# Latents of the last four row tiles on VectorE, up-projection weights and V scales prepared a step ahead

## The chip, the core and the metric

The kernel runs on one core of one Trainium2 chip. A core has TensorE (PE; its weight loads are shown apart as PEld), VectorE (DVE), ScalarE (ACT), GpSimd (POOL) and SyncE (SP, which here issues every DMA). Each engine works through its own queue in order; engines wait for one another through semaphores. On-chip data lie in SBUF (128 partitions), matmul results in eight PSUM banks of 128 x 512 float32. The metric is the device time of one execution in microseconds (us), as the median of several runs.

## The reference

One encoder layer on a sequence of 1024 rows of width 1024, float32:

```python
mod = silu(c) @ w_ada + b_ada                    # shift, scale, gate for both halves
h = rmsnorm(x) * (1 + scale) + shift
q_lat, kv_lat, k_rope, ca_qkv = split(h @ w_in)  # 256, 128, 32, 3*8*64 columns
q  = rmsnorm(q_lat) @ w_q_up                     # 8 heads x 96
kv = rmsnorm(kv_lat) @ w_kv_up                   # 8 heads x (64 key + 64 value)
k  = concat(kv keys, k_rope for every head)      # 96 = 64 + 32
q, k = rmsnorm(q), rmsnorm(k); rotary on the last 32
o_mla = chunk-causal softmax attention(q, k, v)            # 8 heads
o_ca  = banded chunk attention(rmsnorm(cq), rmsnorm(ck), cv) + relative bias   # 8 heads
x = x + gate_a * (concat(o_mla, o_ca) @ w_out)
u = causal depthwise conv(modulated rmsnorm(x) @ w_up)
x = x + gate_m * ((silu(u_gate) * u_val) @ w_down)
```

## The kernel before

Every float32 product is made of three matmuls: a matrix is split into a high part (rounded) and a low part (the remainder), and high x high, high x low and low x high are added in PSUM. `hi_of` makes the high part (line 78 on ACT), `lo_of` the remainder (line 85, on POOL with `"p"`, on DVE with `"v"`). So each weight tile costs a load, one rounding and one subtraction ahead of its matmuls.

The program is written as streams that a scheduler merges. The main stream runs 64 attention tiles of the banded heads (units `c00` to `c31`) and then 64 of the latent heads (`m00` to `m13`): scores on PE (lines 814 and 821), a maximum on DVE, the exponential on ACT (line 846), scaling and splitting of the probabilities on POOL (line 74, tile `hl`) and DVE (line 868), a transposing DMA (line 880, `PT<-hl`), and the product with the values on PE (line 908). Between them a list of generators, the fillers, gives PE other work: `f_v` (values of the banded heads), `f_qk`, `f_m` (the latents), `f_up(0)` and `f_up(1)` (the up-projections of four latent heads each), `f_oca`. A pacing rule decides how many filler steps are recorded behind each attention tile; a list scheduler then puts all instructions into the queue of each engine by priority and by its own estimate of time. So the written order is not the order of the queues, and an edit in one filler moves instructions of its neighbours.

The part in question:

- `f_m` makes the latents in eight row tiles t. Tile `mp_t` is 24 matmuls (128 x 416, lines 155 to 157); ACT copies it into `lat_t` (line 514) and squares it (518 to 520); POOL makes the reciprocal root `mr_t` (lines 521, 120, 121), scales the two latents with it (523, 524) and rotates the shared key part (`rope_apply`, 498 to 501). After four tiles PE transposes the scaled latents, three pages of four blocks (line 531, bank `lt_ps`); ACT and DVE split each page (534, 535) into `latT`. Tag `T` has a single PSUM bank (`TB = 1`); tag `mm` has two.
- `f_up(gr)` loads the two weight tiles `wqr` and the tile `wkr`, splits them into `wq` and `wk` (ACT, then POOL), and makes the scale of the values: a sum of squares on ACT (line 649), then `pow2_scale`, which goes from DVE (323) to PE (325, tile `vspm`), DVE (326), POOL (328) and DVE again. Then for each of eight tiles t: `qu` (six matmuls), `ku` (three), their copies and squares on ACT (667 to 689), sums and rotation on DVE (673 to 695), the roots and the scaled key on POOL (120, 121, 694).
- `f_v(pp)` makes the same kind of scale (`vspc`) for the banded heads' values, after the first projection `ipv`.

Tag `A` is a ring of four SBUF tiles, which `f_ada` (a stream of modulation weights) and the loads of the output weights, `wor`, use; a load into it waits until the tile four allocations earlier has been read.

## Time and profile before

| | |
|---|---|
| runs | 1309.72 us median of 3 (1309.15 to 1316.19) |
| the profiled execution | 1314.38 us, of which the profile's span is 1312.6 us |
| PE busy | 1195.0 us (91%), 6168 matmuls |
| DVE busy | 1071.0 us (82%) |
| ACT, POOL busy | 624.9 us (48%), 600.2 us (46%) |
| TensorE clock granted, mean | 0.963 |

Up to about 600 us the program is attention with its fillers; after 700 us it is the channel half, in which PE is busy throughout. A busy share is an average over both halves: what a change between 60 and 600 us is worth is read from the waits there. The latents `mp` run from 257 to 330 us, the up-projections from 342 to 423 us.

### The profile page before, as it was taken

The numbers are of one execution on the slowest core, as the hardware profiler recorded it, in microseconds if no ns is written. First come the engines' busy times: TensorE is split into PE (matmuls) and PEld (weight loads), VectorE is DVE, ScalarE is ACT, GpSimd is POOL, SyncE is SP. The second block draws the span as 40 slices with busy tenths as digits, with TensorE's granted clock in tenths as the row PEclk, the third lists the DMA queues.
The fourth block names the chain that finished last, engine by engine and source line by source line (L and its number), as shares of the span: only waits on it lengthen the run. The fifth ranks groups of instructions, "written<-read, shape, count | busy, mean of one in ns | idle before, by whom it ended". The sixth has DMA issues, their size and how long they took to land. (4 is left out here: it accounts for less than half of the span.)

```text
span 1312.6 us, 18651 instructions
## 1 busy us (share of the span) xinstructions
PE 1195.0 (91%) x6168; PEld 992.1 (76%) x6168; DVE 1071.0 (82%) x1800; ACT 624.9 (48%) x1148; POOL 600.2 (46%) x639
## 2 busy tenths in 40 slices
PE   4899999989768889968989999999999999999998
PEld 3789888869546667756768888888888886888886
DVE  6979989878589678875899889888888987687667
ACT  5454654455567355543474444444444353433331
POOL 5485873587688544455615444544444441000000
PEclk9899999989889899988999999999999998999999
DMA  8416768666224757889603343333333338943441
GB/s 326 146 52 152 178 144 193 153 157 126 48 75 87 157 132 148 170 165 347 241 0 113 96 129 112 122 126 105 113 113 119 114 105 284 381 129 104 129 161 64
DMA packets 223689, 190.82 MB, mean 145 GB/s; under 512 B 148709, under 2 KB 166373, under 8 KB 223593
## 3 DMA queue, kind: packets, MB, share of 16 engines
q1 hardware_dynamic: 223592, 189.64, 51.3%
q8 instruction: 48, 0.79, 0.3%
q14 instruction: 49, 0.39, 0.1%
HBM read 117.50 MB, written 37.49 MB: 118 GB/s over the span
## 5 line engine op out<-in xcount | busy, mean ns | idle before, releaser
L78 ACT ACTIVATE dnP<-dnr 128x1024 fp32r<-128x1024 f32 x73 | 77.5, 1064 | 117.6 <-PE dnA_P L1484 46.4
L1456 DVE TENSOR_TENSOR dnP<-dnr,dnP 128x1024 fp32r<-128x1024 f32 x72 | 87.9, 1224 | 51.5 <-ACT dnP L78 50.0
L74 POOL TENSOR_SCALAR hlm<-Pm,rim 128x512 f16<-128x512 f32 (+3 forms) x96 | 69.5, 733 | 64.8 <-DVE rim L849 17.9
L85 POOL TENSOR_TENSOR wf<-wu,wf 128x512 fp32r<-128x512 f32 x22 | 38.7, 1758 | 116.3 <-ACT wf L78 116.3
L85 POOL TENSOR_TENSOR wb<-wu,wb 128x512 fp32r<-128x512 f32 x22 | 44.7, 2033 | 84.9 <-ACT wb L78 57.1
L821 PE MATMUL sm<-kp,qp 96*128 96x512 f32 (+7 forms) x288 | 71.2, 375 | 13.2 <-ACT Pm L846 11.8
L868 DVE SCALAR_TENSOR_TENSOR hlm<-Pm,rim,hlm 128x512 f16<-128x512 f32 (+3 forms) x96 | 70.6, 749 | 10.3 <-POOL hlm L74 10.1
L1318 DVE SCALAR_TENSOR_TENSOR u<-c,cvp,u 128x1023 f32<-128x1023 f32 x44 | 55.8, 1309 | 27.6 <-ACT u L1317 26.2
L74 POOL TENSOR_SCALAR hlc<-Pc,ric 128x640 f16<-128x640 f32 (+2 forms) x64 | 49.4, 775 | 44.1 <-DVE ric L849 12.9
L821 PEld LDWEIGHTS sm<-kp,qp 96*128 96x128 f32 (+1 forms) x288 | 49.1, 198 | 25.0 <-ACT Pm L846 16.7
L846 ACT ACTIVATE Pm<-sm,mm 128x128 f32<-128x128 f32 (+3 forms) x64 | 47.3, 739 | 38.8 <-DVE mm L839 23.4
L846 ACT ACTIVATE Pc<-sc,mc 128x640 f32<-128x640 f32 (+2 forms) x64 | 42.2, 660 | 49.4 <-DVE mc L836 28.0
L1317 ACT ACTIVATE u<-c,cvp 128x1024 f32<-128x1024 f32 x44 | 52.3, 1238 | 23.4 <-DVE c L1416 16.5
L868 DVE SCALAR_TENSOR_TENSOR hlc<-Pc,ric,hlc 128x640 f16<-128x640 f32 (+2 forms) x64 | 51.3, 808 | 7.8 <-POOL hlc L74 7.6
L78 ACT ACTIVATE wc<-ws 128x512 fp32r<-128x512 f32 x21 | 13.3, 632 | 92.9 <-DVE ws L1166 87.1
L908 PE MATMUL pvm<-PTm,vt 128*128 128x256 f16 (+1 forms) x320 | 42.9, 281 | 14.7 <-DMA PTm<-hlm 10.9
L155 PE MATMUL ipq<-wq_s,hT 128*128 128x256 f32 x192 | 56.0, 292 | 0.0
L1319 DVE SCALAR_TENSOR_TENSOR u<-c,cvp,u 128x1022 f32<-128x1022 f32 x44 | 55.5, 1300 | 0.0
L157 PE MATMUL ipq<-wq_s,hT 128*128 128x256 f32 x192 | 55.1, 287 | 0.0
L156 PE MATMUL ipq<-wq_s,hT 128*128 128x256 f32 x192 | 55.0, 287 | 0.0
L839 DVE TENSOR_REDUCE mm<-sm 128x1 f32<-128x128 f32 (+3 forms) x64 | 47.3, 746 | 9.3 <-PE sm L821 8.8
L908 PEld LDWEIGHTS <-vt 128*128 128x128 f16 x320 | 30.6, 103 | 28.8 <-issue 11.8
(436 smaller groups left out, 4385.1 us busy)
## 6 DMA issues: line engine op xcount, KB each, us to landing
wu<-w_up SPq DMA_DIRECT2D x44, 512.0 KB, 3.6
dnr<-g_d SPq DMA_DIRECT2D x73, 256.0 KB, 2.7
aw<-w_ada SPq DMA_DIRECT2D x48, 256.0 KB, 3.2
g_d<-u SPq DMA_DIRECT2D x22, 512.0 KB, 3.0
dnr<-w_down SPq DMA_DIRECT2D x44, 256.0 KB, 5.4
adaw<-w_ada_a SPq DMA_DIRECT2D x16, 512.0 KB, 6.1
x<-x SPq DMA_DIRECT2D x16, 512.0 KB, 8.9
g_d<-gs SPq DMA_DIRECT2D x22, 256.0 KB, 2.8
```

Source lines behind the costliest of these rows:

```text
L74: pool.tensor_scalar(o, i, s, 1.0, op0=MUL, op1=MUL)
L78: act.activation(o, i, AF.Copy)
L85: (pool if eng == "p" else dve).tensor_tensor(o, i, f32(hi), op=SUB)
L155: pe.matmul(pt, sh, mh, start=(start and i == 0), stop=False)
L157: last = pe.matmul(pt, sl, mh, start=False, stop=(stop and i == n - 1))
L821: last = pe.matmul(s[:, c:c + w], qpg[a][rr, q], kpgs[kh][rr, b, ko:ko + w], start=(a == 0 and b == 0), stop=(a == 1))
L846: act.activation(pr[:, :n], sv, AF.Exp, bias=m[:], scale=-1.0, accum_out=rsum[:, 0:1])
L868: dve.scalar_tensor_tensor(hl[:, w:2 * w], pp, ri[:], hl[:, :w], op0=MUL, op1=SUB)
L908: last = pe.matmul(dst, u.vst(j), mov, start=(x == 0), stop=(x == len(todo) - 1), skip_group_check=True)
L1318: dve.scalar_tensor_tensor(u[:, 1:], c[:, :S - 1], cvp[:, cv + 1:cv + 2], u[:, 1:], op0=MUL, op1=ADD)
L1319: dve.scalar_tensor_tensor(u[:, 2:], c[:, :S - 2], cvp[:, cv:cv + 1], u[:, 2:], op0=MUL, op1=ADD)
L1456: r = f(*a, **k)
```

## The change

Six edits:

1. `f_v`: `pow2_scale` is recorded ahead of the first projection, not behind it.
2. `f_m`, tiles 4 to 7: the two scalings and the key rotation go from POOL to DVE. `mr_t` stays on POOL.
3. `f_m`, second half: pages 1 and 2 of the transposed latents take banks of tag `mm`; page 0 stays in `T`.
4. A new function `up_prep(gr)` holds the loads of the up-projection weights and the scale of the values. It is called at tile 5 of `f_m` for `gr = 0`, and at tile 5 of `f_up(0)` for `gr = 1`.
5. Its loads go into the four tiles of ring `A`, where before they went into the two of ring `sq`.
6. For `gr = 0` the remainders of the two `wq` tiles are made on DVE, not on POOL.

```diff
         for t in range(0, NT, 2):   # f_v
...
-            pt = ps.tile([P, 512], F32, name=f"ipv{pp}_{t}", tag="mm", bufs=2)
-            yield from proj2(pt, t, w, 256)
             if t == 0:
                 vscale["c", pp] = pow2_scale(f"c{pp}", ssw[:], hb[:], ND, 2.0 * D)
                 sc = vscale["c", pp][0]
+            pt = ps.tile([P, 512], F32, name=f"ipv{pp}_{t}", tag="mm", bufs=2)
+            yield from proj2(pt, t, w, 256)
...
-            pool.tensor_scalar(raw[:, :QR], raw[:, :QR], r[:, 0:1], 1.0, op0=MUL, op1=MUL)
-            pool.tensor_scalar(raw[:, QR:QR + KVR], raw[:, QR:QR + KVR], r[:, 1:2], 1.0, op0=MUL, op1=MUL)
-            rope_apply(kr[:, t:t + 1, :], raw[:, QR + KVR:NM].unsqueeze(1), tabk, t, 1, raw[:, NM:NM + 64])
+            eng = dve if t >= NT // 2 else pool
+            eng.tensor_scalar(raw[:, :QR], raw[:, :QR], r[:, 0:1], 1.0, op0=MUL, op1=MUL)
+            eng.tensor_scalar(raw[:, QR:QR + KVR], raw[:, QR:QR + KVR], r[:, 1:2], 1.0, op0=MUL, op1=MUL)
+            rope_apply(kr[:, t:t + 1, :], raw[:, QR + KVR:NM].unsqueeze(1), tabk, t, 1, raw[:, NM:NM + 64], eng)
             lat[t] = raw
+            if t == NT - 3:
+                up_prep(0)
             if j == 3:
                 for b in range(3):
-                    ptt = ps.tile([P, 512], F32, name=f"lt_ps{h}_{b}", tag="T", bufs=TB)
+                    own = h == 1 and b > 0
+                    ptt = ps.tile([P, 512], F32, name=f"lt_ps{h}_{b}", tag="mm" if own else "T", bufs=2 if own else TB)
...
+    def up_prep(gr):
+        raws = []
+        for k in range(2):
+            raw = atile(f"wqr{gr}_{k}")
+            sp.dma_start(raw[:], I["w_qu"][gr][:, k, :])
+            raws.append(raw)
+        raw = atile(f"wkr{gr}")
+        sp.dma_start(raw[:], I["w_kvu"][gr])
+        raws.append(raw)
+        ssw = cst.tile([P, 1], F32, name=f"sswm{gr}")
+        junk = qtile(f"wkj{gr}")
+        act.activation(junk[:, 0:256].rearrange("p (a b) -> p a b", a=4),
+                       raw[:].rearrange("p (a b) -> p a b", a=4)[:, :, NOPE:], AF.Square, accum_out=ssw[:])
+        vscale["m", gr] = pow2_scale(f"m{gr}", ssw[:], gb2[:], 1, float(KVR))
+        upw[gr] = raws
...
-            raw = qtile(f"wqr{gr}_{k}")
-            sp.dma_start(raw[:], I["w_qu"][gr][:, k, :])
             w = g4([P, 2, 512], F32R, f"wq{gr}_{k}")
-            hi_of("a", w[:, 0], raw[:])
-            lo_of("p", w[:, 1], raw[:], w[:, 0])
+            hi_of("a", w[:, 0], upw[gr][k][:])
+            lo_of("v" if gr == 0 else "p", w[:, 1], upw[gr][k][:], w[:, 0])
             wq.append(w)
...
+            if gr == 0 and t == NT - 3:
+                up_prep(1)
```

What the scheduler makes of it is read from the queues of the two built programs. In the rows the first number of a name is its group or half, the second its tile; the last one is only a label. The queues differ from about 60 us on; from the end of the attention on they are the same.

GpSimd's queue at the end of the latents, before (`mss_7` and `mr_7` are the sums and the reciprocal roots of the last row tile `lat_7`; `wq0`, `wk0` the up-projection weights of group 0):

```order
L521 TENSOR_SCALAR mss_7_4502<-mss_7_4502 128x1
L500 TENSOR_TENSOR kr_93<-lat_7_4499 128x16
L501 TENSOR_TENSOR kr_93<-lat_7_4499 128x16
L120 TENSOR_SCALAR mss_7_4502<-mss_7_4502 128x1
L121 TENSOR_TENSOR mr_7_4503<-mss_7_4502,nhalf_75 128x2
L523 TENSOR_SCALAR lat_7_4499<-lat_7_4499,mr_7_4503 128x256
L524 TENSOR_SCALAR lat_7_4499<-lat_7_4499,mr_7_4503 128x128
L85 TENSOR_TENSOR wq0_0_4568<-wqr0_0_4566,wq0_0_4568 128x512
L85 TENSOR_TENSOR wq0_1_4573<-wqr0_1_4571,wq0_1_4573 128x512
L85 TENSOR_TENSOR wk0_4595<-wkr0_4576,wk0_4595 128x512
```

The same place in the changed program (`wq1`, `wk1` are the weights of group 1, `wo` the output weights):

```order
L121 TENSOR_TENSOR mr_6_4443<-mss_6_4442,nhalf_75 128x2
L85 TENSOR_TENSOR wk0_4595<-wkr0_4361,wk0_4595 128x512
L85 TENSOR_TENSOR wq1_0_4909<-wqr1_0_4787,wq1_0_4909 128x512
L521 TENSOR_SCALAR mss_7_4525<-mss_7_4525 128x1
L120 TENSOR_SCALAR mss_7_4525<-mss_7_4525 128x1
L85 TENSOR_TENSOR wq1_1_4912<-wqr1_1_4789,wq1_1_4912 128x512
L121 TENSOR_TENSOR mr_7_4526<-mss_7_4525,nhalf_75 128x2
L85 TENSOR_TENSOR wk1_4915<-wkr1_4791,wk1_4915 128x512
L85 TENSOR_TENSOR wo4_0_5301<-wor4_0_5299,wo4_0_5301 128x512
L85 TENSOR_TENSOR wo5_0_5306<-wor5_0_5304,wo5_0_5306 128x512
```

The scalings and rotations are gone from this queue, but the root `mr_7` now stands behind the remainder of `wq1_1`, a weight of the next group; five remainders that came later (`wq1_0`, `wq1_1`, `wk1`, `wo4_0`, `wo5_0`) stand here.

ScalarE's queue there, before, from the copy of the last latent tile on (`msq_7` are its squares, `latT1_0` the first page of the second half, `oc31_1` an attention result):

```order
L514 ACTIVATE lat_7_4499<-mp_7_4433 128x416
L518 ACTIVATE msq_7_4501,mss_7_4502<-lat_7_4499 128x256
L519 ACTIVATE msq_7_4501,mss_7_4502<-lat_7_4499 128x128
L520 ACTIVATE msq_7_4501,ssr_94<-lat_7_4499 128x32
L78 ACTIVATE wq0_0_4568<-wqr0_0_4566 128x512
L534 ACTIVATE latT1_0_4521<-lt_ps1_0_4516,pk_65 128x512
L78 ACTIVATE wq0_1_4573<-wqr0_1_4571 128x512
L917 ACTIVATE oc31_1_5066<-pvc31_1_4963,vabc1_2612 64x512
L534 ACTIVATE latT1_1_4545<-lt_ps1_1_4540,pk_65 128x512
```

And in the changed program, right behind that copy:

```order
L78 ACTIVATE wq0_0_4589<-wqr0_0_4357 128x512
L78 ACTIVATE wq0_1_4592<-wqr0_1_4359 128x512
L78 ACTIVATE wk0_4595<-wkr0_4361 128x512
L78 ACTIVATE wq1_0_4909<-wqr1_0_4787 128x512
L518 ACTIVATE msq_7_4524,mss_7_4525<-lat_7_4522 128x256
L519 ACTIVATE msq_7_4524,mss_7_4525<-lat_7_4522 128x128
L520 ACTIVATE msq_7_4524,ssr_94<-lat_7_4522 128x32
L933 ACTIVATE oc31_1_5066<-pvc31_1_4963,vabc1_2486 64x512
L78 ACTIVATE wq1_1_4912<-wqr1_1_4789 128x512
L78 ACTIVATE wk1_4915<-wkr1_4791 128x512
L78 ACTIVATE wo4_0_5301<-wor4_0_5299 128x512
L78 ACTIVATE wo5_0_5306<-wor5_0_5304 128x512
```

Four weight roundings moved ahead of the squares of `lat_7`; four more stand behind them, and `latT1_0` comes only after those.

GpSimd's queue where group 0 of the up-projections ends, before (`hlm` are the probabilities of the first latent head, `uss`, `ur` and `kn` the sums, roots and scaled keys of the up-projections, `vsm1` the scale of group 1's values):

```order
L85 TENSOR_TENSOR wq1_0_4888<-wqr1_0_4886,wq1_0_4888 128x512
L120 TENSOR_SCALAR uss0_7_4865<-uss0_7_4865 128x8
L74 TENSOR_SCALAR hlm00_0_0_4958<-Pm00_0_4954,rim00_0_4947 128x128
L85 TENSOR_TENSOR wq1_1_4893<-wqr1_1_4891,wq1_1_4893 128x512
L121 TENSOR_TENSOR ur0_7_4866<-uss0_7_4865,nhalf_75 128x8
L74 TENSOR_SCALAR hlm00_1_0_5033<-Pm00_1_5029,rim00_1_5022 128x256
L74 TENSOR_SCALAR hlm00_2_0_5049<-Pm00_2_5045,rim00_2_5038 128x384
L85 TENSOR_TENSOR wk1_4915<-wkr1_4896,wk1_4915 128x512
L694 TENSOR_TENSOR kn0_6_4820<-kraw0_7_4874,ur0_7_4866 128x4x64
L85 TENSOR_TENSOR wo4_0_5301<-wor4_0_5299,wo4_0_5301 128x512
L85 TENSOR_TENSOR wo5_0_5306<-wor5_0_5304,wo5_0_5306 128x512
L328 TENSOR_TENSOR vsm1_4901<-vsm1_4901,nhalf_75 128x1
```

And in the changed program:

```order
L85 TENSOR_TENSOR wo6_0_5311<-wor6_0_5309,wo6_0_5311 128x512
L85 TENSOR_TENSOR wo7_0_5316<-wor7_0_5314,wo7_0_5316 128x512
L120 TENSOR_SCALAR uss0_6_4856<-uss0_6_4856 128x8
L121 TENSOR_TENSOR ur0_6_4857<-uss0_6_4856,nhalf_75 128x8
L85 TENSOR_TENSOR wo4_1_5321<-wor4_1_5319,wo4_1_5321 128x512
L74 TENSOR_SCALAR hlm00_2_0_5049<-Pm00_2_5045,rim00_2_5038 128x384
L120 TENSOR_SCALAR uss0_7_4888<-uss0_7_4888 128x8
L710 TENSOR_TENSOR kn0_6_4843<-kraw0_6_4865,ur0_6_4857 128x4x64
L121 TENSOR_TENSOR ur0_7_4889<-uss0_7_4888,nhalf_75 128x8
L74 TENSOR_SCALAR hlm00_3_0_5136<-Pm00_3_5132,rim00_3_5125 128x512
L710 TENSOR_TENSOR kn0_6_4843<-kraw0_7_4897,ur0_7_4889 128x4x64
```

The five remainders have left this stretch for the end of the latents, and `vsm1` stands further ahead, behind the roots of tile 4.

SyncE's queue where the first latent heads overlap with group 1 (`wor` are loads of the output weights, `PTm` the transposes of the probabilities `hlm`), before:

```order
L880 DMA_TRANSPOSE PTm01_0_0_5529<-hlm01_0_0_5526 128x2x128
L704 DMA wor1_0_7485<-w_out 128x512
L880 DMA_TRANSPOSE PTm00_6_1_5467<-hlm00_7_1_5500 128x8x128
L704 DMA wor2_0_7490<-w_out 128x512
L880 DMA_TRANSPOSE PTm01_0_0_5529<-hlm01_1_0_5556 128x4x128
L704 DMA wor3_0_7495<-w_out 128x512
L880 DMA_TRANSPOSE PTm01_2_0_5595<-hlm01_2_0_5592 128x6x128
L716 DMA cl0_5339<-oT_d_60 128x4x128
```

And in the changed program:

```order
L896 DMA_TRANSPOSE PTm00_6_0_5462<-hlm00_7_0_5496 128x8x128
L720 DMA wor1_0_7485<-w_out 128x512
L720 DMA wor2_0_7490<-w_out 128x512
L720 DMA wor3_0_7495<-w_out 128x512
L896 DMA_TRANSPOSE PTm01_0_0_5529<-hlm01_0_0_5526 128x2x128
L896 DMA_TRANSPOSE PTm00_6_1_5467<-hlm00_7_1_5500 128x8x128
L896 DMA_TRANSPOSE PTm01_0_0_5529<-hlm01_1_0_5556 128x4x128
```

The three loads, which wait for free tiles of ring `A`, stood between the transposes and now stand ahead of three of them.

More of the change, by code (lines that the diff above doesn't have):

```diff
@@ L629, in layer_kernel @@
     mq, mk, mv = {}, {}, {}
+    upw = {}
+    def up_prep(gr):
[13 more added lines that the diff above has]
+        upw[gr] = raws
     def f_up(gr):
@@ L638, in f_up @@
         for k in range(2):
-            raw = qtile(f"wqr{gr}_{k}")
-            sp.dma_start(raw[:], I["w_qu"][gr][:, k, :])
             w = g4([P, 2, 512], F32R, f"wq{gr}_{k}")
-            hi_of("a", w[:, 0], raw[:])
-            lo_of("p", w[:, 1], raw[:], w[:, 0])
+            hi_of("a", w[:, 0], upw[gr][k][:])
+            lo_of("v" if gr == 0 else "p", w[:, 1], upw[gr][k][:], w[:, 0])
             wq.append(w)
-        raw = qtile(f"wkr{gr}")
-        sp.dma_start(raw[:], I["w_kvu"][gr])
-        ssw = cst.tile([P, 1], F32, name=f"sswm{gr}")
-        junk = qtile(f"wkj{gr}")
-        act.activation(junk[:, 0:256].rearrange("p (a b) -> p a b", a=4),
-                       raw[:].rearrange("p (a b) -> p a b", a=4)[:, :, NOPE:], AF.Square, accum_out=ssw[:])
-        vscale["m", gr] = pow2_scale(f"m{gr}", ssw[:], gb2[:], 1, float(KVR))
+        raw = upw[gr][2]
         sc = vscale["m", gr][0]
```

## The prediction

> **What bounds the kernel now.** I read the page for the shares, then the busy time by stretch where the change works, then PE's waits there, then the timeline of single instructions. The stretches, in us; the columns are busy time of PE, PEld, DVE, ACT and POOL (instructions in brackets), the granted clock and the DMA share:
>
> ```profile
> span 1312.6 us, 18651 instructions
> 320.00:330.00 10.00, 10.00 (x57) 9.79 (x57) 6.01 (x17) 5.73 (x25) 9.12 (x22) 1.00 0.61 95
> 330.00:342.00 12.00, 6.40 (x38) 4.90 (x36) 3.50 (x6) 6.03 (x16) 9.02 (x16) 0.69 0.54 120
> 379.00:390.00 11.00, 8.35 (x33) 5.77 (x32) 7.61 (x19) 6.20 (x16) 10.84 (x11) 0.85 0.47 126
> 390.00:430.00 40.00, 32.67 (x178) 24.77 (x176) 39.73 (x94) 28.18 (x71) 34.46 (x36) 1.00 0.44 89
> 440.00:600.00 160.00, 135.08 (x758) 105.06 (x757) 118.94 (x257) 78.94 (x163) 69.90 (x88) 0.91 0.77 165
> ```
>
> No one engine bounds this half. PE is full up to 330 us, where the latents end; from 330 to 342 it works 6.40 of 12.00 us. Where group 1 of the up-projections begins, at 379, POOL is the fullest (10.84 of 11.00); from 390 to 430 it is DVE (39.73 of 40.00). So time taken out before 390 is kept only if DVE can start its full stretch earlier; from 379 to 390 it has 11.00 - 7.61 = 3.4 us free. The waits of PE in the two gaps (who waits, for what: sum, times, longest):
>
> ```profile
> PE lt_ps L531 <- POOL lat L523: 4.0, 2, 3.4
> PE lt_ps L531 <- DVE latT L535: 1.6, 1, 1.6
> ...
> PE vspm L325 <- DVE vsm L323: 2.9, 1, 2.9
> ```
>
> The first two are the gap at the end of the latents: the transposes wait for POOL's scaling, then for their one bank. The third is the gap at group 1: PE stands at the value scale `vspm`, and the next `qu` is queued behind it.
>
> **Part 1: `f_v`'s scale ahead of its projection.** In the first call PE waited at its second projection:
>
> ```profile
> 78.50 0.39 PE L155 MATMUL ipv<-wv_s,hT 128*128 128x256 f32 x1 [1.46 <-DVE vsc L326]
> ```
>
> This wait goes. A little comes back, since the scale's matmul now stands where its input is just being made, and all later projections are queued behind it. The edit is worth between -1.5 us and 0 (nothing, if the scores, which start later, wait for something else); I take -1.2, nearest to the row.
>
> **Part 2: the end of the latents.** It is counted from the end of the last latent tile, 329.47 + 0.35 = 329.8 us; `qu` starts at 341.75, 11.9 us later:
>
> ```profile
> 329.47 0.35 PE L157 MATMUL mp<-wm_h,hT 128*128 128x416 f32 x1
> ...
> 329.88 1.26 PE L908 MATMUL pvc<-PTc,v 128*128 128x256 f16 x12
> 331.77 0.33 PE L531 MATMUL lt_ps<-ident,lat 128*128 128x128 f32 x1 [0.63 <-POOL lat L523]
> ...
> 341.46 0.43 PE L325 MATMUL vspm<-vsm,ones 128*128 128x1 f32 x2
> 341.75 0.77 PE L155 MATMUL qu<-wq,latT 128*128 128x512 f32 x1
> ```
>
> Read alone, the edits take away 3.4 us (scaling) and 1.6 us (bank). But the new queues put another chain in their place. POOL's `mr_7` stands behind the remainder of `wq1_1`; that needs its rounding on ACT, this its load, and the load needs a tile of ring `A`, which comes free when DVE has made the remainder of `wq0_0`. The durations:
>
> ```profile
> 329.86 0.52 ACT L514 ACTIVATE lat<-mp 128x416 f32<-128x416 f32 x1 [1.98 <-PE mp L157]
> L78 ACT ACTIVATE wq<-wqr x4: 629/630/631, 332.7 to 373.4; 128x512 fp32r<-128x512 f32 x4
> L85 DVE TENSOR_TENSOR wo<-wor,wo x4: 679/686/693, 574.4 to 595.6; 128x512 fp32r<-128x512 f32 x4
> wor<-w_out SPq DMA_DIRECT2D x16, 256.0 KB, 3.1
> L85 POOL TENSOR_TENSOR wq<-wqr,wq x4: 1262/1264/1273, 335.8 to 375.0; 128x512 fp32r<-128x512 f32 x4
> L121 POOL TENSOR_TENSOR mr<-mss,nhalf x8: 706/708/1225, 287.6 to 334.2; 128x2 f32<-128x2 f32 x8
> L523 POOL TENSOR_SCALAR lat<-lat,mr 128x256 f32<-128x256 f32 x5 | 2.4, 480 | 0.2
> L534 ACT ACTIVATE latT<-lt_ps,pk 128x512 fp32r<-128x512 f32 x6 | 4.1, 686 | 5.4 <-PE lt_ps L531 5.4
> L535 DVE SCALAR_TENSOR_TENSOR latT<-lt_ps,pk,latT 128x512 fp32r<-128x512 f32 x6 | 4.5, 747 | 4.6 <-ACT latT L534 4.5
> ```
>
> From the end of `mp_7`: copy 0.5, rounding of `wq0_0` 0.6, DVE's remainder 0.7, and 0.2 for its turn, my estimate, since the rotation of `lat_7` stands ahead of it: 2.0. Load 3.1, rounding of `wq1_1` 0.6, POOL's remainder 1.3, root 0.7: 7.7. The scaling on DVE has no row; it lies between 0 and twice POOL's 0.48, and I take 0.5, nearest to POOL's row: 8.2. Three transposes at 0.33: 9.2. Pages 0 and 1 on ACT, 0.7 each, then page 1 on DVE, 0.7: 11.3. `qu` needs the bank of page 1, now one of its own two, so it starts at 11.3 instead of 11.9: -0.6.
>
> Against that, what filled PE's pause is now queued ahead of the last two latent tiles: 12 value products (1.26) and `vspm` (0.43). The end of `mp_7` comes 1.7 us later. `vspm` waits there for DVE behind the last exponential of the banded heads, a new wait between 0 and the 2.9 of its row above. Value products and transposes stand between those scores and it and cover most of that: I take 1.0. One small wait of PE goes, as the scores stand further apart:
>
> ```profile
> 317.69 0.56 PE L814 MATMUL sc<-kp,qp 128*128 128x256 f32 x2 [0.52 <-ACT Pc L846]
> ```
>
> The sum is -0.6 + 1.7 + 1.0 - 0.5 = +1.6 us. Its ends: if `mr_7` is not held, 3.4 and 1.6 go, 1.7 comes later, nothing stands at `vspm`, and the 0.5 goes: -3.8. If nothing is gained at `qu` and 2.9 is lost at `vspm`, 1.7 + 2.9 = +4.6. The banks and the preparation do not end this stretch, then; the root does. DVE's added work (eight scalings, sixteen small rotations, two remainders) I cost at nothing: DVE works 6.01 of 10.00 us there and 3.50 of 12.00 behind it. Without that cover it would cost 2 x 0.7 for the remainders and 4 x 0.5 for the scalings, 3.4 us.
>
> A rule speaks against this move. POOL's smaller scaling took 0.93 us at one time and 0.38 at another:
>
> ```profile
> 327.39 0.93 POOL L524 TENSOR_SCALAR lat<-lat,mr 128x128 f32<-128x128 f32 x1
> 335.43 0.38 POOL L524 TENSOR_SCALAR lat<-lat,mr 128x128 f32<-128x128 f32 x1
> ```
>
> The Trainium skill, "SBUF — State Buffer", section "Who interferes with whom", says that VectorE's tensor_scalar can run in two-port modes that take the port pair shared with GpSimd as an exclusive lock, and that its tensor_tensor with both inputs in SBUF holds up GpSimd's reads; the two rows, which differ by 0.55 us for the same work, are of that kind. By that rule the two remainders now on DVE could stop POOL for up to 1.4 us, and the time below would be 1307.1. I don't add it: on the chain above POOL stands idle ahead of `wq1_1`, waiting for its load, and takes such a delay there.
>
> **Part 3: the start of group 1.** Its scale and weights are ready long before; the 2.9 us go, and with them PE's slow restart:
>
> ```profile
> 378.95 0.63 PE L156 MATMUL qu<-wq,latT 128*128 128x512 f32 x1
> 379.37 0.63 PE L157 MATMUL qu<-wq,latT 128*128 128x512 f32 x1
> ...
> 384.52 0.40 PE L156 MATMUL qu<-wq,latT 128*128 128x512 f32 x1
> 384.75 0.40 PE L157 MATMUL qu<-wq,latT 128*128 128x512 f32 x1
> ```
>
> After the gap matmuls start 0.42 us apart, later 0.23; eight of them cost 8 x 0.19 = 1.5 us. Together -4.4 us. POOL loses five remainders of 1.26 here, 6.3 us, which is what lets PE move on; late next are POOL's roots and scaled probabilities. The ends are 0 (DVE, full from 390 on, takes all back) and -7.8 (POOL's 6.3 and the 1.5).
>
> **The sum.** -1.2 + 1.6 - 4.4 = -4.0 us. The profiled execution took 1314.4 us, 1.8 more than its span, and would take 1310.4; it lies 4.7 above the median of 1309.7, and on the median the sum gives 1305.7. Besides, the scheduler re-plans all queues from 60 to 600 us. What that does to waits elsewhere has no row. From 440 to 600 PE stands for 160.00 - 135.08 = 24.9 us; a good quarter of that, 7 us either way, is my spread.
>
> **The rivals.** POOL's relief is worth more. If PE's other waits around 379 go as well, since roots and probabilities come from POOL, part 3 is -4.4 - 1.5 - 1.3 - 1.4 = -8.6 and the time 1301.5. For it speaks POOL's 10.84 of 11.00; against it, that DVE has only 3.4 us free there.
>
> ```profile
> 374.57 0.45 PE L741 MATMUL mq_ps<-ident,qn 128*96 128x128 f32 x1 [1.45 <-DVE qn L692]
> 383.89 0.50 PE L908 MATMUL pvm<-PTm,vt 128*128 128x256 f16 x4 [1.27 <-DMA PTm<-hlm]
> 388.58 0.50 PE L155 MATMUL ku<-wk,latT 128*128 128x512 f32 x1 [1.37 <-ACT uqr L667]
> 421.09 1.24 SPq L880 DMA_TRANSPOSE PTm<-hlm  x1
> ```
>
> Nothing comes of it: DVE's 39.73 of 40.00 takes back part 3, and -1.2 + 1.6 = +0.4 is left, 1310.1.
>
> Slower, by SyncE's queue: the loads `wor1_0` to `wor3_0` now stand ahead of three transposes of probabilities, and each waits for a tile that POOL frees with a remainder of 1.26 us. That holds the transposes for up to 3.8 us; they then leave one behind the other, 3 x 1.24 = 3.7, and PE, whose value products hang on them, restarts slowly, 1.5. So -4.0 + 9.0 = +5.0 and 1314.7; slower than before from a hold of 4.0 us in all on. For it speaks that PE waited 1.27 us for just such a transpose with POOL full; against it, that fewer remainders are left on POOL by then.
>
> **How the numbers follow.** A measurement of this kernel can tell about 0.5%, 6.5 us, from no change: faster is under 1303.2, slower over 1316.2. My forecast, 1305.7, has a chance of 0.40 (its own range 1298 to 1313), the relief 0.28, no effect 0.14, SyncE's queue 0.18. With the spread of 7 us the shares under 1303.2 are 0.36, 0.60, 0.16 and 0.05, together 0.14 + 0.17 + 0.02 + 0.01 = 0.34, and those over 1316.2 are 0.07, 0.02, 0.19 and 0.41, together 0.03 + 0.01 + 0.03 + 0.07 = 0.14. The bounds of parts 2 and 3 reach further down than up, so I say 0.36 for faster, 0.14 for slower and 0.50 between. The range leaves out the last tenth on each side: 1296 to 1317.
>
> **What would show it.** Right: no wait at `vspm` of group 1, and `qu` there at the quick pace; at the end of the latents one wait of PE at `lt_ps` of some 5 us, now for DVE's scaling, and about 11 us from the last `mp` to the first `qu`. Wrong: that distance at 7 us, or waits for `PTm` well over these 10.9 us in all:
>
> ```profile
> PE pvm L908 <- DMA PTm<-hlm: 10.9, 10, 3.0
> ```
>
> The prediction falls if the time from the first `qu` of group 0 to the last `ku` of group 1 does not shrink by some 4 us.

## Result, and the profile after

The change makes the kernel slower: 1323.4 us median of six runs (1319.6 to 1325.1) against 1313.8 for the kernel before, run beside it (1309.2 to 1317.1). The ratio is 1.0075, 95% interval 1.0053 to 1.0097, so about 10 us. The prediction had said 1305.7: 4.0 less than the 1309.7 that the kernel before had taken until then. The profiled execution took 1322.2 us, its span is 1320.4, 7.8 more than before, at nearly the same mean clock (0.961 against 0.963).

The same stretches as before; columns are the width, then the busy time of PE, PEld, DVE, ACT and POOL, the granted clock, the DMA share and GB/s:

```profile
320.00:330.00 10.00, 5.21 (x33) 3.65 (x32) 8.74 (x31) 7.68 (x24) 2.70 (x5) 0.87 0.59 112
330.00:342.00 12.00, 11.44 (x50) 10.62 (x48) 5.69 (x22) 2.39 (x11) 5.31 (x9) 0.68 0.47 56
...
379.00:390.00 11.00, 10.54 (x46) 8.38 (x44) 10.01 (x30) 9.58 (x28) 6.16 (x8) 0.86 0.00 1
390.00:430.00 40.00, 32.86 (x155) 24.13 (x155) 38.02 (x95) 26.65 (x68) 33.78 (x35) 0.91 0.35 73
440.00:600.00 160.00, 136.84 (x778) 107.83 (x778) 125.47 (x278) 81.03 (x168) 71.02 (x96) 0.93 0.77 156
```

The first row holds a loss that the prediction did not price: from 320 to 330 us PE was full before and now works 5.21 of 10.00. The third looks like what was hoped for, POOL down from 10.84 to 6.16 of 11.00 and PE up from 8.35 to 10.54, but it holds other work than before: group 1 now begins at 388.0 us, not at 378.4. Its first 11 us are these:

```profile
388.00:399.00 11.00, 8.48 (x26) 5.02 (x25) 10.08 (x23) 5.72 (x16) 10.66 (x11) 0.69 0.44 107
```

There POOL works 10.66 and PE 8.48, much as before, at a lower granted clock (0.69 against 0.85). PE's waits over the whole program (sum, times, longest):

```profile
PE pvm L924 <- DMA PTm<-hlm: 11.9, 11, 3.0
...
PE pvc L924 <- DMA PTc<-hlc: 11.5, 9, 3.7
...
PE lt_ps L535 <- DVE lat L524: 6.8, 1, 6.8
...
PE mq_ps L757 <- DVE qn L708: 3.1, 1, 3.1
...
PE lt_ps L535 <- POOL lat L524: 1.7, 1, 1.7
...
PE vspm L325 <- DVE vsm L323: 0.7, 2, 0.6
```

Of the 2.9 us at `vspm` of group 1 0.2 are left (the other 0.6 are group 0's), but a wait of 3.1 us at `mq_ps`, the transposes of group 0's scaled rows `qn`, now stands right ahead of it. PE's long wait for the scaling of the last tiles is now one, for DVE, as forecast. PE's instructions at the end of the latents (start, duration, what it waited for):

```profile
320.34 0.35 PE L157 MATMUL mp<-wm_h,hT 128*128 128x416 f32 x1
...
329.04 2.29 PE L924 MATMUL pvc<-PTc,v 128*128 128x256 f16 x12 [3.74 <-DMA PTc<-hlc]
331.12 0.42 PE L535 MATMUL lt_ps<-ident,lat 128*128 128x128 f32 x1
332.11 0.59 PE L325 MATMUL vspm<-vsm,ones 128*128 128x1 f32 x2 [0.56 <-DVE vsm L323]
332.55 0.69 PE L155 MATMUL mp<-wm_h,hT 128*128 128x416 f32 x1
...
343.82 0.35 PE L157 MATMUL mp<-wm_h,hT 128*128 128x416 f32 x1
...
352.91 0.69 PE L535 MATMUL lt_ps<-ident,lat 128*128 128x128 f32 x2 [6.76 <-DVE lat L524]
...
355.61 0.79 PE L155 MATMUL qu<-wq,latT 128*128 128x512 f32 x1 [1.02 <-DVE latT L539]
```

Between `mp_5` (done at 320.7) and `mp_6` (332.55) stand the last banded scores, value products and `vspm`, with waits between them; then the 48 matmuls of the last two tiles run alone, the first ones slowly. The program's landmarks give the account, after minus before: first `mp` +6.1 us (256.8 to 262.9); first to last `mp` +8.2 (73.0 to 81.2); last `mp` to first `qu` -0.5 (11.9 to 11.4); first `qu` to last `ku` -4.9 (81.4 to 76.6). That is +8.9 at the last `ku`, and 7.8 are left at the end. So 6 us are lost ahead of the latents and 8 in them. Only `f_v`'s edit reaches the first part: without it and with the rope tables in their place all queues are the same as before up to about 318 us. Twelve profiled executions with these same queues, the kernel before among them, come to the first `mp` between 255.8 and 259.5 us, the three with both calls edited and nothing else changed there (the changed kernel, e1, e11) between 263.0 and 263.7; so part of the 6 can be chance, but not all.

### The profile page after: what moved, and what is told of

It is laid out like the page before. It is cut to its first block, busy times and chain, and to the rows that moved or that the text cites. A ratio compares the mean times of both kernels' runs of the same rounds, so it can differ in the third digit from the quotient of the medians.

```text
span 1320.4 us, 18652 instructions
## 1 busy us (share of the span) xinstructions
PE 1194.7 (90%) x6168; PEld 993.1 (75%) x6168; DVE 1085.4 (82%) x1826; ACT 625.5 (47%) x1148; POOL 588.3 (45%) x613
## 4 chain that ended last, share of the span: by engine, by line
PE 57%; DVE 18%; DMA 7%; POOL 7%; issue 6%; ACT 4%; SPq 1%; POOLq 0%; ACTq 0%; DVEq 0%
PE p L1163 10%; PE p L1165 10%; PE p L1164 10%; PE dnA_P L1498 2%; PE dnA_P L1499 2%; PE dnA_P L1500 2%; DVE hlc L884 2%; DMA PTm<-hlm 2%; PE dnB_P L1499 2%; PE dnB_P L1500 2%; PE dnB_P L1498 2%; PE sm L837 1%; DMA aw<-w_ada 1%; DVE hlm L884 1%; DVE adacc L279 1%
## 5 line engine op out<-in xcount | busy, mean ns | idle before, releaser
L74 POOL TENSOR_SCALAR hlm<-Pm,rim 128x512 f16<-128x512 f32 (+3 forms) x96 | 66.0, 696 | 74.6 <-DMA PTm<-hlm 18.3
L1334 DVE SCALAR_TENSOR_TENSOR u<-c,cvp,u 128x1023 f32<-128x1023 f32 x44 | 58.6, 1372 | 27.6 <-ACT u L1333 27.6
L837 PE MATMUL sm<-kp,qp 96*128 96x512 f32 (+7 forms) x288 | 68.6, 367 | 12.0 <-ACT Pm L862 11.9
L862 ACT ACTIVATE Pc<-sc,mc 128x640 f32<-128x640 f32 (+2 forms) x64 | 42.2, 660 | 76.6 <-DVE mc L852 51.7
L884 DVE SCALAR_TENSOR_TENSOR hlm<-Pm,rim,hlm 128x512 f16<-128x512 f32 (+3 forms) x96 | 66.2, 704 | 11.0 <-POOL hlm L74 10.6
L837 PEld LDWEIGHTS sm<-kp,qp 96*128 96x128 f32 (+1 forms) x288 | 48.4, 196 | 23.3 <-ACT Pm L862 17.7
L924 PE MATMUL pvm<-PTm,vt 128*128 128x256 f16 (+1 forms) x320 | 45.2, 288 | 19.6 <-DMA PTm<-hlm 11.9
L1335 DVE SCALAR_TENSOR_TENSOR u<-c,cvp,u 128x1022 f32<-128x1022 f32 x44 | 61.7, 1443 | 0.0
```

What stands on the lines that cost most here:

```text
L74: pool.tensor_scalar(o, i, s, 1.0, op0=MUL, op1=MUL)
L837: last = pe.matmul(s[:, c:c + w], qpg[a][rr, q], kpgs[kh][rr, b, ko:ko + w], start=(a == 0 and b == 0), stop=(a == 1))
L862: act.activation(pr[:, :n], sv, AF.Exp, bias=m[:], scale=-1.0, accum_out=rsum[:, 0:1])
L884: dve.scalar_tensor_tensor(hl[:, w:2 * w], pp, ri[:], hl[:, :w], op0=MUL, op1=SUB)
L924: last = pe.matmul(dst, u.vst(j), mov, start=(x == 0), stop=(x == len(todo) - 1), skip_group_check=True)
L1335: dve.scalar_tensor_tensor(u[:, 2:], c[:, :S - 2], cvp[:, cv:cv + 1], u[:, 2:], op0=MUL, op1=ADD)
```

## The experiments

Medians in us; the ratio is to the kernel before, with the 95% interval. For progress inside a run I use the times of the exponentials. Where an expectation speaks of tile 28 of the banded heads, it is record 28 of them; each exponential leaves two records, so it is the fifteenth of 64.

**Which edit loses?** e1 is the kernel before with `f_v`'s edit alone, e2 with the scaling and rotation on DVE alone (`eng`), e3 with `up_prep` alone (loads in ring `A`, remainders on POOL), e4 the changed kernel without `f_v`'s edit.

```diff
 # e1, on before
+            if t == 0: vscale["c", pp] = pow2_scale(...)     # now ahead of proj2, both calls
 # e2, on before
+            eng = dve if t >= NT // 2 else pool
 # e3, on before
+            if t == NT - 3: up_prep(0)                       # f_m; up_prep(1) in f_up(0)
 # e4, on after
-            if t == 0: vscale["c", pp] = pow2_scale(...)     # back behind proj2
```

> The kernel before with f_v's edit alone: the value scale stands ahead of the first projection, in both calls. Theory A (the loss is a new plan that this edit causes: with it alone the queues already differ from the first value projection on, and in the changed kernel the last value projection of v1 ran 6.1 us later than before): 1320 us, 6 us over the kernel before (1313.8), with the last ipv and the last ipq some 6 us late. Theory B (the loss comes from the latents: scaling and key rotation on VectorE): 1312 to 1314, as the prediction's part 1 had it (-1.2). Theory C (the early preparation causes it): 1312 to 1314 too.

> The kernel before with the last four latent tiles' scaling and key rotation on VectorE alone; all queues keep their order but for some 30 rows at the latents. Theory A: 1310.4 to 1314, the 3.4 us of PE's wait for GpSimd's scaling go or another wait takes their place. Theory B: 1320 to 1324, VectorE (full for long stretches) delays exponentials and scores there, and the distance from the first lt_ps to the last mp grows by several us. Theory C: 1310.4 to 1314.

> The kernel before with the early preparation alone: raw weights of the up-projections in ring A, loads, value scales and their sums of squares issued at latent tile 5 and at tile 5 of group 0; scaling, key rotation and remainders stay on GpSimd, f_v and the banks as before. Theory A: 1309.4, part 3 of the prediction (-4.4) with nothing against it. Theory B: the same, 1309.4. Theory C: 1322 to 1324, the loads and the scale's matmul in the latents' queues make the latents later by 8 us or more, and part 3 gives 4 back.

> The changed kernel without f_v's edit: all others stay. Theory A: 1313 to 1317, some 6 to 10 us under the changed kernel's 1323.4, with the latents and group 0 where the prediction had them (first qu at 343 us instead of 355.6). Theory B and theory C: 1323 to 1325, no gain from leaving it out, and the distance from the first mp to the last mp stays near 80 us (73 before).

| | median | ratio |
|---|---|---|
| e1 | 1318.8 | 1.0035 (1.0020 to 1.0050) |
| e2 | 1316.8 | 1.0013 (1.0000 to 1.0027) |
| e3 | 1327.5 | 1.0100 (1.0076 to 1.0124) |
| e4 | 1318.1 | 1.0033 (1.0018 to 1.0047) |

`f_v`'s edit costs 4.7 us alone, and 5.3 by the difference of the changed kernel and e4. The other edits together cost the remaining 4. Theory A holds for half of the loss; theory B falls (DVE's scaling and rotation alone cost between 0 and 3.5 us by the interval, though theory A had expected no loss from them at all). Theory C holds in a form that was not foreseen: the preparation alone costs 13.5 us, and the edits beside it take most of that back. In e3 and e4 the first up to the last `mp` takes 79.5 and 77.3 us, against 73.0. The rest of e3's loss comes behind the up-projections, whose last `ku` is as early as before (423.7 us against 423.2).

The theories are told apart by which of their ranges a run comes nearest to. Their sizes were poor: here and below the totals of e3, e5, e11, e12 and e17 lie 3.5 to 9 us outside everything that was expected of them.

**Why does the early preparation cost so much?** In the changed kernel, e3 and e4 `vspm` of group 0 is recorded at latent tile 5 and takes one of the two banks of tag `mm`, ahead of `mp_6`; and `mp_6` and `mp_7` come behind it on PE. e5 moves the matmul of both value scales into the transposes' bank, e9 that of group 0 alone, e10 that of group 1 alone, e11 both in the whole changed kernel; e6 records group 0's scale behind the last latent tile.

```diff
 # e5, on e4 (e9: nm == "m0"; e10: nm == "m1"; e11: on after)
-        pt = ps.tile([P, 512], F32, name=f"vsp{nm}", tag="mm", bufs=2)
+        pt = ps.tile([P, 512], F32, name=f"vsp{nm}", tag="T" if nm[0] == "m" else "mm", ...)
 # e6, on e4: the scale leaves up_prep(0), the loads stay
+            if t == NT - 1: up_scale(0)
```

> All edits but f_v's (1318.1 us), and the matmul of both value scales of the up-projections (vspm) writes to the single bank of the transposes instead of to one of the two that the latent tiles use. Theory D (mp_6 and mp_7 are planned behind vspm of group 0, because it takes its bank in program order ahead of mp_6 and its input comes late; so the 48 matmuls that filled PE's waits among the last banded scores run alone at the end): in this order mp_6 again stands between the last banded scores; the time from the last banded exponential to the first exponential of group 0 shrinks by 4 to 6 us and the total is 1312 to 1314. Rival E (what is late at the end of the latents is the root and VectorE's scaling, whatever PE does before it): 1317 to 1319, the first qu at 348 us as before this edit.

> All edits but f_v's (1318.1 us), with group 0's loads still issued at latent tile 5 but its sum of squares and value scale after the last latent tile. Theory D: as the run with the other bank, 1311 to 1314, since mp_6 is planned between the scores again. Rival E: 1317 to 1319. If only the moment of vspm counts and not the order of mp_6, nothing changes either.

> All edits but f_v's (1318.1 us), with the scale's matmul of group 0 alone in the transposes' bank; group 1's stays in the latent tiles' banks. e5, with both moved, took 1302.9. Theory D0 (the order of mp_6 and mp_7 ahead of vspm of group 0 is what counts): 1303 to 1306, nearly all of the gain. Theory D1 (most of it comes from group 1's matmul: in the transposes' bank it holds back the first page transposes of group 0, mq_ps, which otherwise stand between the up-projections and make PE wait for VectorE's qn; in e5 PE's wait for qn is 0.8 us against 4.1): 1313 to 1315, the 3.9 us that e5 gains up to the last mp and no more.

> All edits but f_v's (1318.1 us), with the scale's matmul of group 1 alone in the transposes' bank; group 0's stays, so mp_6 and mp_7 are still planned behind it. Theory D0: 1316 to 1318. Theory D1: 1306 to 1309, PE's wait at mq_ps for qn falls from 4.1 us to about 1, and the up-projections of both groups end some 6 us earlier than in e4; the last mp stays at 337 us.

> The changed kernel whole, f_v's edit in it (1323.4 us), with the matmuls of both value scales of the up-projections in the transposes' bank. If the two losses are independent, e5 plus what f_v's edit costs: 1302.9 + 4.7 = 1307.6 us (5.3 by the difference between the changed kernel and e4: 1308.2), and so under the kernel before all the same. Rival (the delay that f_v's edit causes among the banded heads is swallowed by the waits at the latents once mp_6 and mp_7 fill them): 1303 to 1304. Rival (the plan with f_v's edit has no room for mp_6 between the scores): 1318 to 1323.

| | median | ratio |
|---|---|---|
| e5 | 1302.9 | 0.9919 (0.9894 to 0.9944) |
| e6 | 1317.1 | 1.0022 (1.0004 to 1.0039) |
| e9 | 1306.5 | 0.9947 (0.9928 to 0.9966) |
| e10 | 1320.5 | 1.0049 (1.0032 to 1.0065) |
| e11 | 1313.1 | 0.9998 (0.9982 to 1.0014) |

The bank of one matmul is worth 11.6 us (e4 to e9); with both matmuls moved it is 10.2 in the whole changed kernel (e11). Between D0 and D1 the totals decide for D0: group 0's matmul alone gains 11.6 of the 15.2 us that both together gain on e4 (e5), group 1's alone gains nothing (e10 is 2.5 us slower than e4). What D1 said of group 1 is there all the same: with its matmul moved, group 0 of the up-projections takes 26.8 and 26.9 us from its first `qu` to its last `ku` (e5, e10) instead of 32.4 and 32.2 (e9, e4). Of these 5 us e5 keeps 3.6 over e9, with intervals that overlap, and e10 none. PE in e4, around `vspm` of group 0, and its stretch from 320 to 330:

```profile
325.69 0.38 PE L325 MATMUL vspm<-vsm,ones 128*128 128x1 f32 x2
...
336.38 0.35 PE L157 MATMUL mp<-wm_h,hT 128*128 128x416 f32 x1
```

```profile
320.00:330.00 10.00, 8.00 (x32) 6.66 (x31) 8.24 (x33) 5.30 (x21) 6.14 (x10) 0.68 0.42 80
```

And the same in e9:

```profile
328.97 0.28 PE L325 MATMUL vspm<-vsm,ones 128*128 128x1 f32 x2
...
330.69 0.35 PE L157 MATMUL mp<-wm_h,hT 128*128 128x416 f32 x1
```

```profile
320.00:330.00 10.00, 10.00 (x62) 9.80 (x60) 9.50 (x34) 7.14 (x29) 5.93 (x12) 1.00 0.49 80
```

In e4 all 48 matmuls of `mp_6` and `mp_7` come behind `vspm`; in e9 39 of them come ahead of it, fill the waits among the last scores, and PE is full at the full clock. From the first to the last `mp` e9 takes 73.4 us against 77.3; in the whole changed kernel the same move brings 81.2 down to 74.6 (e11), and PE's idle time within it from 15.0 to 7.5 us, where the kernel before has 8.2. So the stage that the early preparation had lengthened is mended by the bank, by 4 and by 6.6 us.

That is not the whole of 11.6 and 10.2. The first exponential of the latent heads is 5 us earlier in e9 than in e4, and 1.7 of these stand already at the first `mp`, where the queues are still the same. The lead is between 2 and 7 us through most of the latent heads (nothing at one tile) and 8 at their last exponential. The two profiled executions end 13 us apart; behind the last exponential all runs take between 726 and 734 us, so the last 5 can be chance. What makes the lead grow behind the latents is not shown.

One run does not fit. In e6 `mp_6` and `mp_7` stand among the scores too, the first to the last `mp` takes 72.2 us, and the first exponential is even 8 us earlier than in e4. Yet this lead is gone by 460 us, 5 us of it are back at the last exponential of an execution that is the quickest of its twelve, 4 us under the median, and the median is only 1 us under e4's, in rival E's range and not in theory D's. So the order of `mp_6` and `mp_7` explains the stage; that it explains the total is not shown, and why e6 gives its lead back stays open.

**What is DVE's share worth with the preparation?** e12 is e5 with scaling, rotation and group 0's remainders all back on POOL; e15 has only the remainders back, e16 the pages back in one bank. e7 is the kernel before with group 1's preparation alone.

```diff
 # e12, on e5
-            eng = dve if t >= NT // 2 else pool              # and lo_of("p", ...) as in e15
 # e15, on e5
-            lo_of("v" if gr == 0 else "p", w[:, 1], ...)
+            lo_of("p", w[:, 1], ...)
 # e16, on e5
-                    own = h == 1 and b > 0
+                    own = False
 # e7, on before: up_prep(1) in f_up(0), up_prep(0) at the head of f_up(0)
```

> Early preparation with its matmuls in the transposes' bank, and the pages in three banks; the last four tiles' scaling and key rotation and group 0's remainders stay on GpSimd, f_v as before. e2 gave 1.7 us of loss for the move to VectorE alone. If that move is a cost wherever it stands: 1300 to 1301. If it pays once the preparation gives GpSimd remainders to make at the end of the latents (PE then waits for GpSimd's scaling as in e3, 11 us in two waits, against 2.9 for VectorE's in e5): 1306 to 1312.

> e5 (1302.9 us) with group 0's two weight remainders back on GpSimd; scaling and key rotation of the last four tiles stay on VectorE. e12, with all three back on GpSimd, took 1321.0. If the remainders are what pays (the chain of the prediction's part 2: the root of the last tile stands behind a remainder on GpSimd): 1312 to 1321. If the scaling and the rotation are what pays: 1303 to 1306.

> e5 (1302.9 us) with the last pages of the latents in their one bank again, as before the change. If the banks are worth the wait that they were made for (1.6 us at lt_ps for latT): 1304 to 1305. If, with the scale's matmul and the pages in the same bank, they are what keeps the first up-projection from waiting: 1308 to 1312. If nothing hangs on them: 1303.

> The kernel before with group 1's preparation alone made early (at tile 5 of group 0); group 0's stands where it stood, f_v, the latents' scaling and the banks as before. The prediction's part 3 alone: -4.4 us, 1309.6, with no wait at vspm of group 1 and nothing lost up to the first qu. Rival (what is won at the start of group 1 is taken back behind it by scores and transposes of group 0 that are planned otherwise): 1313 to 1316. Rival by SyncE's queue (the loads of w_out stand ahead of transposes): over 1316.

| | median | ratio |
|---|---|---|
| e12 | 1321.0 | 1.0064 (1.0042 to 1.0085) |
| e15 | 1303.8 | 0.9935 (0.9916 to 0.9954) |
| e16 | 1305.3 | 0.9940 (0.9924 to 0.9957) |
| e7 | 1311.5 | 0.9981 (0.9966 to 0.9997) |

PE's wait for the scaling in e3, e12 and e15, in this order:

```profile
PE lt_ps L533 <- POOL lat L523: 11.0, 2, 7.2
```

```profile
PE lt_ps L534 <- POOL lat L523: 8.5, 1, 8.5
```

```profile
PE lt_ps L535 <- DVE lat L524: 6.0, 1, 6.0
```

With the weights prepared early, scaling and rotation on DVE are worth 17 us (e12 to e15), although by themselves they gain nothing (e2). Early preparation gives POOL the remainders to make just when the last tiles want scaling, but that is only a small part of the 17: from e12 to e15 PE's wait falls from 8.5 us to 6.0, with another 0.5 at the second scaling, and the time from the last `mp` to the first `qu` from 18.2 to 14.7. The first exponential of the latent heads is 4 us earlier; from 465 us on the lead is between 8 and 17 us, and which waits give that is not shown. The remainders' place is worth nothing that shows, the banks 2.5 us, with intervals that overlap. e7 gains 2.1 us; its trace doesn't show where. PE still waits 1.9 us at `vspm` of group 1 in it, against the forecast of none, and the last `ku` comes when it came before (423.0 us against 423.2).

**Why does `f_v`'s edit lose?** e8 has it in the first call alone, on the kernel before; e13 in the second alone, on e5; e14 is e11 with `vspc` in the value products' bank too. e17 is the kernel before with the rope tables (a filler on DVE) driven by `qk2` instead of `qk1`, e18 the same with e8's edit.

```diff
 # e8, on before (e13: pp == 1, on e5)
+            if t == 0 and pp == 0: vscale["c", pp] = pow2_scale(...)   # ahead of proj2
 # e14, on e11
+        pt = ps.tile([P, 512], F32, name=f"vsp{nm}", tag="T" if nm[0] == "m" else "pv", bufs=1)
 # e17, on before; e18, on e8
-            if key == "qk1":
+            if key == "qk2":          # rope_tables() steps
```

> The kernel before with f_v's edit in the first call alone (e1, with both calls, took 4.7 us more than before). Theory F (the first call's edit does it: the page transposes of the first unit and the scores behind it are planned in another order, and e1 was 5 us late by the seventh banded unit already, long before the second call): 1318 to 1320, with tile 28 of the banded heads 4 to 5 us late. Rival (the second call does it): 1313 to 1315, tile 28 not late.

> e5 (1302.9 us: all edits but f_v's, the scales' matmuls of the up-projections in the transposes' bank), with f_v's edit in the second call alone. e8 (first call alone) took 8.5 us more than before, e1 (both calls) 4.7. If the second call gains what these two differ by: 1299 us. If its new plan is a loss like the first call's: 1307 to 1311. If it does nothing: 1303.

> The changed kernel whole with the matmuls of all value scales out of the latent tiles' banks: those of the up-projections in the transposes' bank as in e11 (1313.1 us), those of f_v in the bank of the value products. Theory bank (f_v's edit loses as the early preparation does, because vspc takes a bank ahead of the projections): 1303 to 1305. Theory VectorE (the scale's small operations and the first qn and minima come in another order on VectorE, which is full there, and each minimum of a score waits behind fillers): 1311 to 1315, with tile 28 of the banded heads again 4 to 6 us late.

> The kernel before with the steps that make the rope tables on VectorE driven by the third projection (qk2) instead of the second (qk1), so that VectorE is less full between 95 and 135 us. Base for e18. If the tables make the first banded scores late as it is: tile 28 of the banded heads 2 to 5 us earlier and 1309 to 1312 us. If the later projection has no more room: 1313 to 1318.

> e17 with f_v's edit in the first call. Theory VectorE (the edit loses because VectorE is full there and puts remainders and rope steps ahead of the minima of the scores): with the tables out of the way tile 28 is within 1 us of e17's, and the total within 2 us of e17's. Rival (the new order loses by itself, by the page transposes that stand earlier in PE's queue): tile 28 is 4 us later than in e17, and the total 5 to 8 us over e17's.

| | median | ratio |
|---|---|---|
| e8 | 1322.1 | 1.0064 (1.0041 to 1.0086) |
| e13 | 1308.0 | 0.9975 (0.9955 to 0.9994) |
| e14 | 1314.3 | 1.0007 (0.9992 to 1.0022) |
| e17 | 1322.9 | 1.0074 (1.0048 to 1.0100) |
| e18 | 1328.4 | 1.0118 (1.0092 to 1.0143) |

Each call costs 5 us or more where it is made alone (e8: 8.5, e13: 5.2 over e5). Both together cost 4.7 on the kernel before (e1) and 10.3 on e5 (e11): what the new order costs depends on the queues that it meets. It is not the bank that the projections rotate through: with `vspc` out of it the total gains nothing (e14: 1.1 over e11), and the fifteenth exponential is as late as in e11 (148.7 us against 147.5; 141.8 before). (The bank it went to may cost something of its own: the first `mp` of e14 comes 8 us behind e11's.) What is seen of it: the wait that the edit took away comes back 8 us later. The transposes of the second query page, before (first row) and in the changed kernel (second):

```profile
85.69 0.63 PE L741 MATMUL q_ps<-ident,qn 128*128 128x128 f32 x4 [0.30 <-DVE qlow L774]
```

```profile
86.58 0.63 PE L757 MATMUL q_ps<-ident,qn 128*128 128x128 f32 x4 [1.61 <-DVE qlow L790]
```

The scores hang on these pages, which hang on the roots, and not on the value projections; so the first exponential comes no earlier (88.55 us before, 88.43 in e8). Behind it DVE is full; the third busy time is DVE's, in the kernel before:

```profile
100.00:135.00 35.00, 32.73 (x265) 31.25 (x264) 34.05 (x107) 16.17 (x34) 20.05 (x23) 1.00 0.66 155
```

In e8 DVE works 33.09 of these 35.00 us, no more than before, but in another order. ACT's waits there, from 86 to 148 us, before and in e8:

```profile
ACT Pc L846 <- DVE mc L836: 9.4, 8, 3.0
...
ACT Pc L846 <- DVE ric L849: 0.2, 1, 0.2
```

```profile
ACT Pc L849 <- DVE mc L839: 11.8, 5, 6.0
...
ACT Pc L849 <- DVE ric L852: 4.1, 3, 2.8
...
ACT Pc L849 <- DVE rt L557: 2.6, 1, 2.6
...
ACT Pc L849 <- DVE ric L851: 1.4, 1, 1.4
...
ACT Pc L849 <- DVE hlc L871: 0.7, 1, 0.7
```

The exponentials' waits for DVE grow from 9.6 to 20.6 us, and the fifteenth exponential is late by 4.2:

```profile
141.83 0.80 ACT L846 ACTIVATE Pc<-sc,mc 128x640 f32<-128x640 f32 x1
```

```profile
146.06 0.79 ACT L849 ACTIVATE Pc<-sc,mc 128x640 f32<-128x640 f32 x1
```

Whether a full DVE is the cause is not settled. With the rope tables moved out of the way (e17) that exponential comes 6.7 us earlier than before, so they do delay it, and the first call's edit then makes it 1.6 us late instead of 4.2 (e18); but e18 still takes 5.5 us more than e17, and e17 is slower than before itself: it falls back from the sixteenth exponential on, in the projection that now has the tables. That fits neither side: the exponential's 1.6 us are nearer to what theory VectorE expected, the total's 5.5 are what its rival expected. So it is shown that the edit gains nothing at the first scores and where the delay is first seen, not that DVE makes it.

## Why the prediction was wrong

The change was forecast to take 4.0 us away and adds 9.5. (Another 4.1 of the 17.7 us between 1305.7 and 1323.4 lie in the base: the kernel before took 1309.7 in the runs on record and 1313.8 beside the changed one.) The sum was -1.2 + 1.6 - 4.4. Two of its terms failed, part 1 and, in part 2, what stands ahead of the last two latent tiles. Measured on the trace, in its steps:

- **Part 3 gave the right number, but not by its working.** From the first `qu` to the last `ku` the trace shows -4.9 us where -4.4 was given: no long wait at `vspm`, and `qu` at the quick pace at the head of group 1. But the whole pause between the last `ku` of group 0 and the first `qu` of group 1 has gone, 8.6 us before, where the working took 2.9 and 1.5. Against that group 0 takes 32.5 us instead of 28.0: PE waits 3.1 us at `mq_ps` in it and restarts slowly there. Group 1 takes 44.2 us against 44.8. The relief of POOL, which was to let PE move on, is not there: 10.66 of the first 11.00 us of group 1, against 10.84.
- **Part 2, the distance from the last `mp` to the first `qu`, came out right by luck in its sizes**: 11.4 us where 11.3 was worked out against 11.9 before, and PE's long wait is for DVE. The order of the chain holds, and the root is ready after 7.3 us (7.7 forecast). The working took one scaling at 0.5 us; there are two, and they took 2.6 (below). Transposes and splits, taken one behind the other at 3.1 us, ran in part beside the second scaling, and `qu` started 1.6 us after its end. The two errors cancel. DVE's added work at nothing was near the mark (e2, e15).
- **Part 2, the end of `mp_7`, is one step that failed.** What "is now queued ahead of the last two latent tiles", 12 value products and `vspm`, was priced as their work, 1.7 us, and a wait at `vspm`, 1.0, less 0.5 for a wait that goes: 2.2. The working asked what comes ahead of `mp_6` and `mp_7` and not what these two had been covering. They were PE's filler for the waits among the last banded scores. Without them those waits stand open (3.74 us at one value product alone), and PE starts again at a low clock (0.68 granted from 330 to 342 us; before, the two tiles ran at 1.00): its `mp` matmuls of line 155 last 421 ns there, 356 before.

```profile
L155 PE MATMUL mp<-wm_h,hT 128*128 128x416 f32 x16 | 6.7, 421 | 0.0
```

```profile
L155 PE MATMUL mp<-wm_h,hT 128*128 128x416 f32 x16 | 5.7, 356 | 0.0
```

  The rows are of the changed kernel and of the one before. Instead of 2.2 the stage from the first to the last `mp` grew by 8.2 us, 6.8 of them idle time of PE; with the matmuls of the scales in another bank (e11) 6.6 of the 8.2 are gone. That value products and transposes "cover most" of the wait at `vspm` was right in the letter, and the same mistake: `vspm` waits little, and the value products that cover it wait themselves.
- **Part 1 is the other step that failed.** "Worth between -1.5 us and 0": it cost 4.7 to 5.3, and 10.3 on e5; why is open, as said above. The reading that the scores might wait for something else was right. The error was to bound the edit by the wait that it removes while letting the new plan of 500 us of queues stand as 0, 7 us either way. A centre above 0 would have been nearer: PE was busy for 184 of the 200 us from 60 to 260 before, so a new order there had little to win. That is an argument from one row; no run tests it.
- **The rivals.** Slower was expected by SyncE's queue. That isn't it: PE's waits for `PTm` are 11.9 us against 10.9. POOL's relief and DVE's fullness did not decide either. DVE stopping POOL, weighed at up to 1.4 us, cost next to nothing at the chain's place: DVE's two remainders ran from 345.3 to 346.6 us while POOL stood idle until 346.4, and its next remainder took 1.33 us instead of 1.26. The mechanism that made the stage at the latents longer, a small matmul that takes one of two rotating banks ahead of the filler, was not among them, though the new order of PE stood in the text.

The best version found is e5: the change without `f_v`'s edit and with the scales' matmul in the transposes' bank, 1302.9 us, 10.7 under the kernel before; e15 and e16, 0.9 and 2.5 us slower, can't be told from it.

## What to carry to other kernels

When work is queued ahead of a filler, price the waits that the filler was covering, not the work that was put ahead of it: read the stretch with the filler taken out. A preparation that is made early takes a bank, a ring slot and an engine's turn at the new place; give its one small matmul a bank that the main stream does not rotate through, and try it alone in each bank before it is judged. An edit that removes a wait of 1.5 us on an engine whose successors hang on something else gained nothing here, and still changed every queue behind it. And when a change shifts a stage in time, compare the stage with itself by its landmarks: the same window of the clock can hold other work.

## What the runs showed of the hardware

Here DVE's scaling was held up beside POOL's remainders, for about as long as one of them lasts. In the changed kernel the scaling of the seventh tile (first two rows) had POOL idle beside it; that of the last tile (next two) ran beside POOL's remainders, whose rows follow:

```profile
342.14 0.35 DVE L524 TENSOR_SCALAR lat<-lat,mr 128x256 f32<-128x256 f32 x1 [1.31 <-POOL mr L121]
342.40 0.28 DVE L525 TENSOR_SCALAR lat<-lat,mr 128x128 f32<-128x128 f32 x1
...
351.50 1.35 DVE L524 TENSOR_SCALAR lat<-lat,mr 128x256 f32<-128x256 f32 x1 [2.28 <-POOL mr L121]
352.77 1.28 DVE L525 TENSOR_SCALAR lat<-lat,mr 128x128 f32<-128x128 f32 x1
```

```profile
351.44 1.26 POOL L85 TENSOR_TENSOR wk<-wkr,wk 128x512 fp32r<-128x512 f32 x1
352.66 2.54 POOL L85 TENSOR_TENSOR wo<-wor,wo 128x512 fp32r<-128x512 f32 x2
```

0.35 and 0.28 us become 1.35 and 1.28: each DVE instruction starts just after one of POOL's and ends 0.1 us or so behind it. e4, e9 and e15 show the same pair of durations at the same place. The prediction had weighed only the other direction, DVE stopping POOL. The Trainium skill, "SBUF — State Buffer", section "Who interferes with whom", says that VectorE in a two-port mode contends with GpSimd, and that whoever issues first gets the shared pair for the whole instruction while the other fully blocks. These rows agree, with 1.0 us for each of the two; which mode the scalings ran in they don't show. No run here took POOL's remainders from behind the last root, so what these 2 us are worth in the total was not tried.
